# Six units of a mixer kernel with one more Strassen step each, and an earlier, split convolution epilogue

## The chip, the cores and the metric

The kernel runs on one core of one Trainium2 chip. The metric is the device time of that core in microseconds (us); the time of the kernel before is the median of three runs. A profile is of one execution, and its times count from the start of the profiled span.

## The reference

A decoder block on 256 tokens with a model width D of 4096, all in float32. A wide projection feeds two mixers of width 2048, a multi-scale causal pooling mixer and a gated short convolution, which are merged by sigmoid gates and projected out:

```
h    = rmsnorm(x, norm_w)
u_p, z_p, u_c, b_c, c_c, z_c, g = split(h @ w_in)     # 4096 -> 6 x 2048 + 2 x 4096
y_pool = (mix_g(trailing_mean_w(u_p) - u_p) * pool_scale) * silu(z_p)   # windows 2, 4, 8, 16
v      = c_c * u_c
y_conv = (b_c * (conv_b + sum_k conv_w[k] * shift(v, k))) * silu(z_c)   # 3 taps
merged = sum_n sigmoid(g_n + gate_b_n) * (y_n @ w_branch[n])            # n = pool, conv
out    = rmsnorm(x + merged @ w_out, final_norm_w)
```

## The kernel before, in words

**Units and steps.** The work is a list of units, each 1024 columns of a product's output. In order of time they are cz0 cb0 cu0 cc0, cz1 cb1 cu1 cc1 (the convolution's four projections, two halves), pz0 pu0 pz1 pu1 (the pooling's two), eight gate units that begin with g0_0 and end with g1_0, eight branch units b0_0 b1_0 ... b0_3 b1_3, and four output units o0 to o3. A unit of the wide products sums over 4096 rows in 16 steps of 256 rows; a branch unit has 8 steps. Each step is one block of weights, 256 rows by 1024 columns, that SP's queue fetches into `raw`, with an operand that stands on chip: the turned activations for the same 256 rows.

**Products in three.** Every float32 matrix is split into a rounded part (fp32r) and the rest, and a product of two takes three matmuls: high by high, high by low, low by high (L378). A matmul here is 128x512 by a 128x128 weight load. A step is of one of two kinds. P (plain) takes the 2 x 2 x 2 block products one by one: 8 x 3 = 24 matmuls. S (Strassen) takes seven products of sums of blocks: 7 x 3 = 21 matmuls. The order of an S step's products is written out in `groups`: N5 M2 N3 M1 N6 N7 N4; where S is the last step of a unit (`closing`) it is M2 N3 N4 M1 N7 N5 N6. N6, N4 and N7 use the sums of weight blocks that have to be formed first.

**Preparation.** A step's weights are prepared by two engines. ACT rounds the blocks into the ring, 26 cells of 128x512 (`highs`; its rows read ring<-raw and ring<-parts). DVE subtracts to get the rests (`lows`; ring<-raw,ring and ring<-parts,ring), and in an S step also forms the sums (`added` makes parts<-raw and parts<-raw,parts, `split` their rests). P takes 8 cells of the ring, S takes 14; where the cells wrap around the end of the ring, an operation is cut in two. An S step's fourth block (the corner) gets a second DMA of 256 KB on POOL's queue that adds a neighbour block to it (`issue_corner`). `pump` lets preparation run at most four steps ahead of TensorE (AHEAD) and issues a load when the buffer of the step four before is prepared; everything is recorded in program order on every engine.

**What sets the order.** A string of P and S for each unit, such as TEN = "PSPSSPSSPSSPSSPS", says which of its steps are Strassen steps. A unit's epilogue (activation, transposes, moves to DRAM) is a list of items in a queue. After each group of matmuls, `after_group` runs one item for every TICK = 6 matmuls; this count goes on across units. None in the list (`gap(n)` is n of them) lets ticks pass. So an item's place among the preparation steps on DVE and ACT is set by how many matmuls came before it. The convolution's epilogue `c_epi` belongs to cc0 and cc1 and runs while the next unit does, cz1 and pz0: it fetches the silu gate Y, transposes E on TensorE, lets 5 ticks pass, transposes Y, runs the taps (ACT, then `stt` on DVE at L76), and multiplies E = J * Y in one operation of 128x2048.

**Filling operands.** The operands of the branch and output units come back from DRAM by ACT's queue into the staging tiles sa, sb, sc, and are written into `arena` by the ticks (class `Fill`, `queue_fills`): for an S step's operand four sums on DVE (sb<-sb, 128x128 each), a rounding on ACT, and a subtraction on DVE (arena<-sb,arena, 896 or 1024 columns; 512 for a P step's). An operand can be filled once the steps that used its place are done. The order of the fills is the order in which the first unit that uses them, b0_0, b1_0 or o0, takes its steps.

In the views, TensorE's matmuls of steps are on L1063, DVE's tensor-tensor operations on L64 and ACT's on L61, since helpers record them; `sums` and `shared` are the two sets of four PSUM banks.

Of the kernel before, what the change touches and what calls it, by code (L numbers as in the profile page):

```python
# [18 lines left out]
HALF = D // 2  # L19
NU = 1024  # L20
# [12 lines left out]
WARM = 18  # L33
TAIL = 3

SIX5 = "PPPPPSPSPSPSPSPS"
FIRST = (0, 1, 8, 2, 9, 3, 10, 11, 4, 12, 13, 5, 14, 6, 15, 7)
OPENED = 12
SEVEN3 = "PPPSPSPSPSPSPSPS"
NINE = "PSPSPSPSSPSPSSPS"  # L40
NINE_A = "PSPSSPSPSSPSPSPS"
NINE_P = "PSPSSPSPSSPSSPSP"
HOST = "PPBPPMMPSSSPSSSPSSS"
SEVEN5 = "PPPPPSPSPSSPSSPS"
TEN = "PSPSSPSSPSSPSSPS"
OUT3 = "PSPSPSPSPSPSSPPP"
B0 = "PPPPSPSP"
B1 = "PSPSPSPP"
B1_FIRST = "PPSPSPSP"
B0_MORE = "PPPPSSPS"  # L50
# [3 lines left out]
def hybrid_block(ctx: ExitStack, tc: tile.TileContext, x, xc, prm, rows_in, w_in, pool_w, w_branch, w_out, out):  # L54
# [29 lines left out]
    def move(dst, src):  # L84
        return pin(nc.scalar.dma_start(dst, src))
# [410 lines left out]
    def gap(n):  # L496
        return [None] * n
# [68 lines left out]
    def conv_units(c, first):  # L566
        base = 2 * HALF + c * NU

        def b_epi(u):
            def product(t):  # L570
                stt(E[:, t], E[:, t], rin[:, t:t + 1], Y[:, t], ALU.mult, ALU.mult)
            return gap(15) + [lambda: product(0), None, lambda: product(1)] + gap(5) + [lambda: move(g_d[c], E)]

        def c_epi(u):
            def inner(j):
                if j == 3:
                    for i in range(4):
                        act(chan(E)[:, 2 * i:2 * i + 2], bankview(i))

            def outer(j):  # L580
                act(chan(J)[:, 2 * j:2 * j + 2], bankview(j))

            def taps(j):
                v, y = chan(E)[:, 2 * j:2 * j + 2], chan(Y)
                for i in range(2):
                    b = 2 * j + i
                    kb = 8 * c + b
                    act(y[:, b], v[:, i], AF.Identity, scale=tap_col(2, kb), bias=bias_col(kb))
                for s in (1, 2):
                    for i in range(2):  # L590
                        b = 2 * j + i
                        kb = 8 * c + b
                        stt(y[:, b, s:], v[:, i, 0:T - s], tap_col(2 - s, kb), y[:, b, s:], ALU.mult, ALU.add)

            items = gap(2) + [lambda: move(Y, g_d[c])] + gap(6) + pairs(transposes(E, inner)) + gap(5) + pairs(transposes(Y, outer))
            for j, n in enumerate((1, 3, 3, 3)):
                items += gap(n) + [lambda j=j: taps(j)]
            return items + [None, lambda: mul(chan(E), chan(J), chan(Y))] + gap(5) + [lambda: put(y_d[1, c], chan(E))]

        u = in_unit(f"cz{c}", base + 3 * HALF, lambda u: silu_y(u.late) + (gap(4) + side_items(ND - 1) + side_items(ND - 2) if first else []),  # L600
                    FIRST if first else SEVEN5, dst=Y)
        u.late = not first
        in_unit(f"cb{c}", base + HALF, b_epi, TEN if c else NINE_A).late = True
        u = in_unit(f"cu{c}", base, lambda u: rescale(Y), TEN, dst=Y)
        u.late = True
        in_unit(f"cc{c}", base + 2 * HALF, c_epi, TEN).urgent = lambda: mul(E, E, Y)

    def pool_units(c):
        u = in_unit(f"pz{c}", HALF + c * NU, lambda u: silu_y(True) + gap(4) + band_items(c), HOST if c else SEVEN5, dst=Y)
        u.late = True  # L610
        in_unit(f"pu{c}", c * NU, lambda u: [], NINE_P).urgent = lambda: None

# [94 lines left out]
    def gate_unit(n, c):  # L707
        first, final = (n, c) == (0, 0), (n, c) == (1, 0)

        def epi(u):  # L710
            d = u.dst

            def bias(t):
                gather(d[:, t], gate_b[n, None, c * NU:(c + 1) * NU].to_broadcast([P, NU]))

            def gate(t):
                act((spare() if final else d)[:, t], d[:, t], AF.Sigmoid)

            items = (rescale(d) if u.late else gap(1)) + [lambda: bias(0), None, None, lambda: bias(1)] + gap(12) + [
                lambda: gate(0), None, lambda: gate(1)]  # L720
            return items if first or final else items + gap(5) + [lambda: move(gates_d[n, c], E)]
        text = HOST if first else SEVEN3 if final else TEN
        u = in_unit(f"g{n}_{c}", 6 * HALF + n * D + c * NU, epi, text, dst=Y if first else E)
        u.late = not final

# [3 lines left out]
    def branch_unit(n, c):  # L729
        def epi(u):  # L730
            if n == 0:
                if c:
                    return gap(4) + [lambda: move(spare(), gates_d[1, c])] + gap(8) + [lambda: mul(Y, E, Y)]
                return gap(12) + [lambda: mul(Y, E, Y)]
            turned = spare() if c < 3 else Y

            def gated():
                mul(E, E, spare())
                if c == 3:
                    last_pair["stack"].close()  # L740
                    open_last(F32R)
                    last_pair["again"] = True

            def copy(j):
                act(chan(turned)[:, 2 * j:2 * j + 2], bankview(j))

            def stored():
                put(m_d[c], chan(turned))
                merged[c] = now[0] + STORED
            return gap(2) + [gated, None, lambda: add(E, E, Y), None,  # L750
                ] + gap(4) + pairs(transposes(E, copy)) + [
                    lambda: c < 3 and move(Y, gates_d[0, c + 1])] + gap(4) + [stored]

        text = (B1 if c else B1_FIRST) if n else B0_MORE if c else B0
        u = Unit(f"b{n}_{c}", lambda i: w_branch[n, c, i], seq_y(text), y_ops[n], epi)
        u.late = n == 0
        if not u.late:
            u.urgent, u.lead = (lambda: None), 3
        units.append(u)
# [3 lines left out]
    def out_unit(c):  # L763
        cs = slice(c * NU, (c + 1) * NU)

        def start():
            move(Y[:, 0], final_w[None, cs].to_broadcast([P, NU]))

        def epi(u):
            def row(t):  # L770
                gather(E[:, t], xrows[:, t, cs])

            def square(t):
                act(Y[:, 1], E[:, t], AF.Square, accum_out=ossq[:, t, c:c + 1])
            return gap(6) + [lambda: row(0), None, lambda: row(1)] + gap(3) + [start] + gap(11) + [
                lambda: square(0), None, lambda: square(1),
                lambda: mul(E, E, Y[:, 0:1].to_broadcast([P, 2, NU]))] + gap(4) + [lambda: move(o_d[c], E)]

        text = (SIX5, NINE, NINE, OUT3)[c]
        u = Unit(f"o{c}", lambda i: w_out[c, i], seq_x(text), m_ops, epi, before=start if c == 3 else None)  # L780
        u.late = c < 3
        units.append(u)
# [499 lines left out]
```

## Time and profile before

| what | before |
|---|---|
| median of three runs (lowest, highest) | 2353.83 us (2353.54, 2355.73) |
| the profiled execution, its span | 2353.71 us, 2352.0 us |
| TensorE (PE) busy | 2334.8 us, 99% of the span, 10400 matmuls |
| VectorE (DVE) busy | 2110.9 us, 90% |
| ScalarE (ACT) busy | 1528.8 us, 65% |
| GpSimd (POOL) busy | 293.1 us, 12% |
| DMA, mean | 269 GB/s, 633.01 MB |
| chain that ended last | PE 97%, DVE 1%, DMA 1% |

How to read it: the span is the time from the first to the last recorded instruction; an engine's busy time counts its working instructions, not those that issue DMAs. A row of the timeline has a start in us, a duration, the engine, the line, the operation, output <- inputs with shapes, a count, and in brackets the idle time just before it with what ended that. A row of the waits has the engine and its operation, the releaser, and then the sum of the waits in us, their number, and the longest. A row of the windows has the window's limits and length and then, for PE, PEld (weight loads), DVE, ACT and POOL, busy us with the number of instructions, the granted TensorE clock and the busy share of the DMA engines. The granted clock is 1.00 or just under it everywhere.

### The profile page before, as it was taken

How to read it: one execution, taken by the hardware profiler on the slowest of the kernel's cores; microseconds unless marked ns; L12 is line 12 of the kernel's file. 1: busy time of each engine (PE TensorE's matmuls, PEld its weight loads, DVE VectorE, ACT ScalarE, POOL GpSimd, SP SyncE). 2: the span in 40 equal slices, each digit the busy share in tenths (PEclk: the TensorE clock that was granted, in tenths of full speed). 3: DMA queues.
4: the chain of work that ended last, by engine and by line, in shares of the span. 5: the costliest groups of instructions: out<-in, count | busy, mean ns of one | idle time of the engine just before them, and what ended most of it. 6: DMA issues, size and time to landing. Idle time of an engine off the chain costs nothing.

```text
span 2352.0 us, 29771 instructions
## 1 busy us (share of the span) xinstructions
PE 2334.8 (99%) x10400; PEld 1931.9 (82%) x10400; DVE 2110.9 (90%) x2126; ACT 1528.8 (65%) x1897; POOL 293.1 (12%) x356
## 2 busy tenths in 40 slices
PE   9999999999999999999999999999999999999998
PEld 7888888888887888888888888888888888888886
DVE  8789998999989979979999899998898889999988
ACT  6666666666666666667666666666676566666664
POOL 0111100111101101101121111111011010011110
PEclk9999999999999999999999999999999999999999
DMA  9889877989977868868999999999889889889997
GB/s 377 245 249 295 269 235 238 277 243 288 270 231 231 255 203 256 252 207 256 295 276 273 303 284 285 277 312 278 285 259 288 272 253 304 270 235 303 283 264 288
DMA packets 202822, 633.01 MB, mean 269 GB/s; under 512 B 21296, under 2 KB 29744, under 8 KB 199856
## 3 DMA queue, kind: packets, MB, share of 16 engines
q1 hardware_dynamic: 134624, 485.42, 58.7%
q0 software_dynamic: 50400, 103.83, 24.2%
q10 hardware_dynamic: 17648, 41.87, 5.0%
q8 instruction: 81, 1.33, 0.2%
q14 instruction: 69, 0.57, 0.1%
HBM read 583.85 MB, written 25.17 MB: 259 GB/s over the span
## 4 chain that ended last, share of the span: by engine, by line
PE 97%; DVE 1%; DMA 1%; ACT 0%; issue 0%; SPq 0%; DVEq 0%; ACTq 0%
PE sums L1063 69%; PE shared L1063 26%; PE shared L692 1%; PE shared L477 1%; DMA raw<-in_w_in_dram 1%; ACT ring L61 0%; DVE parts L64 0%; DVE ring L64 0%; DVE Y L76 0%; PE shared L668 0%; PE shared L669 0%; PE shared L671 0%; SPq L79 0%; ACT Y L61 0%; PE shared L670 0%
## 5 line engine op out<-in xcount | busy, mean ns | idle before, releaser
L1063 PE MATMUL sums<-ring,arena 128*128 128x512 f32 x6873 | 1640.9, 390 | 4.7 <-DVE ring L64 4.2
L1063 PEld LDWEIGHTS sums<-ring,arena 128*128 128x128 f32 x6873 | 1287.2, 188 | 274.3 <-DVE ring L64 6.8
L64 DVE TENSOR_TENSOR ring<-raw,ring 128x1536 fp32r<-128x1536 f32 (+2 forms) x978 | 1088.4, 1138 | 146.5 <-PE sums L1063 49.3
L61 ACT ACTIVATE ring<-raw 128x512 fp32r<-128x512 f32 (+1 forms) x943 | 900.5, 1015 | 114.7 <-PE sums L1063 89.3
L61 ACT ACTIVATE ring<-parts 128x512 fp32r<-128x512 f32 (+1 forms) x478 | 389.2, 827 | 524.5 <-DVE parts L64 459.7
L1063 PE MATMUL shared<-ring,arena 128*128 128x512 f32 x2283 | 580.8, 389 | 0.2 <-DVE ring L64 0.2
L1063 PEld LDWEIGHTS shared<-ring,arena 128*128 128x128 f32 x2283 | 428.4, 188 | 89.6 <-DVE ring L64 0.6
L64 DVE TENSOR_TENSOR ring<-parts,ring 128x1536 fp32r<-128x1536 f32 (+2 forms) x262 | 404.7, 1555 | 15.8 <-ACT ring L61 8.1
L91 POOL DMA_DIRECT2D raw<-in_w_in_dram x176 | 152.2, 865 | 1375.7 <-DMA raw<-in_w_in_dram 535.7
L64 DVE TENSOR_TENSOR parts<-raw,parts 128x1024 f32<-128x1024 f32 x230 | 280.4, 1219 | 0.0
L64 DVE TENSOR_TENSOR parts<-raw 128x512 f32<-128x512 f32 x230 | 158.1, 687 | 2.7 <-DVE ring L64 0.7
L64 DVE TENSOR_TENSOR J<-J 128x512 f32<-128x512 f32 (+1 forms) x90 | 78.3, 870 | 15.5 <-ACT J L61 13.0
L1063 PE MATMUL sums<-ring,last_pair 128*128 128x512 f32 x306 | 76.5, 389 | 0.0
L61 ACT ACTIVATE J<-shared 128x512 f32<-128x512 f32 x128 | 68.5, 621 | 11.6 <-PE shared L1063 7.2
L61 ACT ACTIVATE E<-sums 128x512 f32<-128x512 f32 x76 | 42.1, 598 | 46.9 <-PE sums L1063 46.0
L1063 PEld LDWEIGHTS sums<-ring,last_pair 128*128 128x128 f32 x306 | 57.4, 188 | 12.0
L1063 PE MATMUL shared<-ring,side 128*128 128x512 f32 x261 | 66.0, 389 | 0.0
L91 POOL DMA_DIRECT2D raw<-in_w_out_dram x31 | 27.0, 872 | 264.9 <-DMA raw<-in_w_out_dram 112.7
L1063 PEld LDWEIGHTS shared<-ring,side 128*128 128x128 f32 x261 | 49.0, 188 | 10.2
L91 POOL DMA_DIRECT2D raw<-in_w_branch_dram x23 | 20.0, 870 | 288.9 <-DVE ring L64 104.1
L1063 PE MATMUL shared<-ring,last_pair 128*128 128x512 f32 x216 | 54.8, 389 | 0.0
L1063 PEld LDWEIGHTS shared<-ring,last_pair 128*128 128x128 f32 x216 | 40.5, 188 | 8.4
(123 smaller groups left out, 682.0 us busy)
## 6 DMA issues: line engine op xcount, KB each, us to landing
raw<-in_w_in_dram SPq DMA_DIRECT2D x318, 768.0 KB, 7.0
raw<-in_w_in_dram SPq DMA_DIRECT2D x326, 256.0 KB, 5.9
raw<-in_w_branch_dram SPq DMA_DIRECT2D x64, 768.0 KB, 6.7
raw<-in_w_out_dram SPq DMA_DIRECT2D x64, 768.0 KB, 6.6
raw<-in_w_in_dram POOLq DMA_DIRECT2D x176, 256.0 KB, 6.8
raw<-in_w_branch_dram SPq DMA_DIRECT2D x64, 256.0 KB, 5.5
raw<-in_w_out_dram SPq DMA_DIRECT2D x64, 256.0 KB, 5.6
E<-J POOLq DMA_DIRECT2D x30, 512.0 KB, 10.0
```

The costliest lines, as they stand in the source:

```text
L61: return pin(nc.scalar.activation(dst, src, func, **kw))
L64: return pin(nc.vector.tensor_tensor(out=dst, in0=a, in1=b, op=op))
L91: return pin(nc.gpsimd.dma_start(dst, src, accum_op=ALU.add))
L477: pin(nc.tensor.transpose(shared(j)[:, i * T + t * P:i * T + (t + 1) * P], src[:, t, c:c + P], ident))
L692: pin(nc.tensor.matmul(o, a, b, start=(k, i) == (0, 0), stop=(k, i) == (3, 2)))
L1063: pin(nc.tensor.matmul(ps, lhs, rhs, start=n == 0, stop=n == u.total[b] - 1))
```

## The change

Six strings are changed, each by one more S in the place of a P. For cz1 and pz0, "PPPPPSPSPSSPSSPS" becomes "PPPPSPSPSSPSSPSS"; the last gate unit g1_0 goes from "PPPSPSPSPSPSPSPS" to "PPPSPSPSPSSPSPSS"; o0 from "PPPPPSPSPSPSPSPS" to "PPPPPSPSPSSPSSPS"; o3 from "PSPSPSPSPSPSSPPP" to "PSPSSPSPSSPSSPPP"; and the first branch unit b0_0 from "PPPPSPSP" to "PPPPSSPS". The operands follow: in b0_0 the fifth, sixth and eighth step are now S steps, and an operand of o0 that was a P step's is an S step's. In `c_epi` the pause ahead of the transposes of Y is one tick and not five, and the product E = J * Y is two operations of 128x1024, two ticks apart.

```
-SEVEN3 = "PPPSPSPSPSPSPSPS"
+EIGHT3 = "PPPSPSPSPSSPSPSS"
...
-SEVEN5 = "PPPPPSPSPSSPSSPS"
+EIGHT4 = "PPPPSPSPSSPSSPSS"
...
-            items = gap(2) + [lambda: move(Y, g_d[c])] + gap(6) + pairs(transposes(E, inner)) + gap(5) + pairs(transposes(Y, outer))
+            items = gap(2) + [lambda: move(Y, g_d[c])] + gap(6) + pairs(transposes(E, inner)) + gap(1) + pairs(transposes(Y, outer))
...
-            return items + [None, lambda: mul(chan(E), chan(J), chan(Y))] + gap(5) + [lambda: put(y_d[1, c], chan(E))]
+            def whole(i):
+                b = slice(4 * i, 4 * i + 4)
+                mul(chan(E)[:, b], chan(J)[:, b], chan(Y)[:, b])
+
+            return items + [None, lambda: whole(0), None, None, lambda: whole(1)] + gap(5) + [lambda: put(y_d[1, c], chan(E))]
...
-                    FIRST if first else SEVEN5, dst=Y)
+                    FIRST if first else EIGHT4, dst=Y)
...
-        u = in_unit(f"pz{c}", HALF + c * NU, lambda u: silu_y(True) + gap(4) + band_items(c), HOST if c else SEVEN5, dst=Y)
+        u = in_unit(f"pz{c}", HALF + c * NU, lambda u: silu_y(True) + gap(4) + band_items(c), HOST if c else EIGHT4, dst=Y)
...
-        text = HOST if first else SEVEN3 if final else TEN
+        text = HOST if first else EIGHT3 if final else TEN
...
-        text = (B1 if c else B1_FIRST) if n else B0_MORE if c else B0
+        text = (B1 if c else B1_FIRST) if n else B0_MORE
...
-        text = (SIX5, NINE, NINE, OUT3)[c]
+        text = (SEVEN5, NINE, NINE, OUT3)[c]
```

(SEVEN5 and B0_MORE keep the strings that they have in the kernel before.) The helper lines move up by one: DVE's L64 and L76 are L63 and L75 after the change, ACT's L61 is L60.

What this does to the order of instructions is shown at two places. The first is DVE's order in pz0, from the last taps (Y<-E,par,Y) over the mul (E<-J,Y) to the rests of the step's sums (ring<-parts,ring); cz1 has the same piece. Before:

```order
L76 SCALAR_TENSOR_TENSOR Y<-E,par,Y 128x254 x2
L64 TENSOR_TENSOR E<-J,Y 128x2048
L64 TENSOR_TENSOR parts<-raw 128x512
L64 TENSOR_TENSOR ring<-raw,ring 128x512
L64 TENSOR_TENSOR parts<-raw,parts 128x1024
L64 TENSOR_TENSOR ring<-raw,ring 128x1536
L64 TENSOR_TENSOR ring<-parts,ring 128x1536
```

After:

```order
L75 SCALAR_TENSOR_TENSOR Y<-E,par,Y 128x254 x2
L63 TENSOR_TENSOR E<-J,Y 128x1024
L63 TENSOR_TENSOR parts<-raw 128x512
L63 TENSOR_TENSOR ring<-raw,ring 128x512
L63 TENSOR_TENSOR parts<-raw,parts 128x1024
L63 TENSOR_TENSOR E<-J,Y 128x1024
L63 TENSOR_TENSOR ring<-raw,ring 128x1536
L63 TENSOR_TENSOR ring<-parts,ring 128x1536
```

The second half of the mul has moved behind the first three operations of the S step, and stands ahead of its two wide ones.

The second is DVE's order near the end of o0: the last S steps' preparation, and with it the filling of the last operands (sb<-sb are the sums of one, arena<-sb,arena its rest). Before:

```order
L64 TENSOR_TENSOR ring<-raw,ring 128x1536
L64 TENSOR_TENSOR ring<-parts,ring 128x1536
L64 TENSOR_TENSOR sb<-sb 128x128 x4
L64 TENSOR_TENSOR ring<-raw,ring 128x1536
L64 TENSOR_TENSOR ring<-raw,ring 128x512
L64 TENSOR_TENSOR parts<-raw 128x512
L64 TENSOR_TENSOR ring<-raw,ring 128x512
L64 TENSOR_TENSOR parts<-raw,parts 128x1024
L64 TENSOR_TENSOR ring<-raw,ring 128x1536
L64 TENSOR_TENSOR ring<-parts,ring 128x1536
L64 TENSOR_TENSOR arena<-sb,arena 128x896
```

After:

```order
L63 TENSOR_TENSOR ring<-parts,ring 128x512
L63 TENSOR_TENSOR sb<-sb 128x128 x4
L63 TENSOR_TENSOR ring<-raw,ring 128x1536
L63 TENSOR_TENSOR ring<-raw,ring 128x512
L63 TENSOR_TENSOR parts<-raw 128x512
L63 TENSOR_TENSOR ring<-raw,ring 128x512
L63 TENSOR_TENSOR parts<-raw,parts 128x1024
L63 TENSOR_TENSOR ring<-raw,ring 128x1536
L63 TENSOR_TENSOR ring<-parts,ring 128x1536
L63 TENSOR_TENSOR arena<-sb,arena 128x1024
```

The rows are the same but for the last, which writes 1024 columns where it wrote 896, and for the wrap of the first.

More of the change, by code (lines that the diff above doesn't have):

```diff
@@ L34 @@
 TAIL = 3
-SIX5 = "PPPPPSPSPSPSPSPS"
+SEVEN5 = "PPPPPSPSPSSPSSPS"
 FIRST = (0, 1, 8, 2, 9, 3, 10, 11, 4, 12, 13, 5, 14, 6, 15, 7)
 OPENED = 12
-SEVEN3 = "PPPSPSPSPSPSPSPS"
+EIGHT3 = "PPPSPSPSPSSPSPSS"
 NINE = "PSPSPSPSSPSPSSPS"
@@ L43 @@
 HOST = "PPBPPMMPSSSPSSSPSSS"
-SEVEN5 = "PPPPPSPSPSSPSSPS"
+EIGHT4 = "PPPPSPSPSSPSSPSS"
 TEN = "PSPSSPSSPSSPSSPS"
-OUT3 = "PSPSPSPSPSPSSPPP"
-B0 = "PPPPSPSP"
+OUT3 = "PSPSSPSPSSPSSPPP"
 B1 = "PSPSPSPP"
```

## The prediction

> **What bounds the kernel now.** I read the page's totals first, then TensorE's waits, then the chain of waits. A change of 0.2% of this kernel, 4.7 us, is about what its measurement can tell from none.
>
> ```profile
> span 2352.0 us, 29771 instructions
> PE 2334.8 (99%) x10400; PEld 1931.9 (82%) x10400; DVE 2110.9 (90%) x2126; ACT 1528.8 (65%) x1897; POOL 293.1 (12%) x356
> PE sums L1063 <- DVE ring L64: 4.2, 3, 1.8
> PE shared L1063 <- DVE ring L64: 0.2, 1, 0.2
> 1591.54 16.32 PE sums L1063 x72
> ```
>
> TensorE is busy for 99% of the span. All of its waits for rounded operands sum to 4.4 us, each for DVE's writes to the ring. The last row is a piece of the chain: 72 matmuls in 16.32 us, 0.2267 us from one to the next. So the time is the number of matmuls times 0.2267 us, plus TensorE's waits, and DVE at 90% decides whether there are more of them.
>
> The stages that change, one row each (cz1, pz0, g1_0, b0_0, o0, o3): the window, its length, then busy PE, PEld, DVE, ACT, POOL, the granted clock, the DMA share:
>
> ```profile
> 336.06:423.34 87.28, 86.22 (x397) 71.31 (x395) 76.45 (x82) 55.25 (x75) 8.59 (x10) 1.00 0.79 240
> 664.06:752.68 88.62, 86.59 (x396) 71.21 (x395) 76.35 (x80) 55.44 (x74) 8.61 (x10) 1.00 0.79 238
> 1591.38:1673.66 82.28, 82.28 (x364) 68.13 (x363) 69.48 (x74) 54.52 (x66) 10.34 (x11) 1.00 0.96 293
> 1673.66:1715.82 42.16, 42.16 (x187) 34.91 (x186) 36.67 (x44) 30.38 (x40) 4.33 (x5) 1.00 0.83 259
> 2011.73:2096.54 84.81, 84.81 (x383) 70.34 (x382) 76.67 (x90) 53.23 (x66) 6.96 (x8) 1.00 0.82 250
> 2258.38:2340.80 82.42, 82.42 (x364) 67.94 (x362) 74.36 (x76) 47.75 (x61) 8.60 (x9) 1.00 0.86 273
> ```
>
> DVE is idle for 5.5 us in b0_0 and for 8 to 13 us in the others. Only cz1 and pz0 leave TensorE idle (1.1 and 2.0 us).
>
> **What a step costs.** The last stretch of o0 shows a P step and an S step on DVE:
>
> ```profile
> 2057.88 1.01 DVE L64 TENSOR_TENSOR sb<-sb 128x128 f32<-128x128 f32 x4
> 2058.80 1.01 DVE L64 TENSOR_TENSOR sc<-sc 128x128 f32<-128x128 f32 x4
> ...
> 2060.05 2.36 DVE L64 TENSOR_TENSOR ring<-raw,ring 128x1536 fp32r<-128x1536 f32 x2 [0.24 <-issue]
> 2064.12 1.23 DVE L64 TENSOR_TENSOR arena<-sb,arena 128x1024 fp32r<-128x1024 f32 x1 [1.71 <-ACT arena L61]
> ...
> 2082.95 2.35 DVE L64 TENSOR_TENSOR ring<-raw,ring 128x1536 fp32r<-128x1536 f32 x2
> 2085.22 0.68 DVE L64 TENSOR_TENSOR parts<-raw 128x512 f32<-128x512 f32 x1
> 2085.82 0.68 DVE L64 TENSOR_TENSOR ring<-raw,ring 128x512 fp32r<-128x512 f32 x1
> ...
> 2089.23 1.75 DVE L64 TENSOR_TENSOR ring<-parts,ring 128x1536 fp32r<-128x1536 f32 x1
> 2090.90 1.08 DVE L64 TENSOR_TENSOR arena<-sb,arena 128x896 fp32r<-128x896 f32 x1
> ```
>
> P takes DVE from 2082.95 to 2085.22, 2.27 us; S from 2085.22 to 2090.90, 5.68 us. Each of the six steps that turn from P to S therefore saves TensorE 3 matmuls (24 to 21), 0.68 us, and loads DVE with 3.41 us more. All six together save 18 x 0.2267 = 4.08 us, 0.17%. The rest of the sum is waits.
>
> [...]
>
> **cz1 and pz0.** TensorE's waits lie in the second S of a pair (step 10), in cz1 (first two rows) and pz0 (the rest):
>
> ```profile
> 392.06 0.84 PE L1063 MATMUL shared<-ring,arena 128*128 128x512 f32 x3
> 394.18 1.42 PE L1063 MATMUL sums<-ring,arena 128*128 128x512 f32 x5 [1.06 <-DVE ring L64]
> 720.16 0.39 PE L1063 MATMUL shared<-ring,arena 128*128 128x512 f32 x1
> 720.73 0.72 PE L1063 MATMUL shared<-ring,arena 128*128 128x512 f32 x2 [0.19 <-DVE ring L64]
> 721.30 0.40 PE L1063 MATMUL sums<-ring,arena 128*128 128x512 f32 x1
> 723.54 1.43 PE L1063 MATMUL sums<-ring,arena 128*128 128x512 f32 x5 [1.84 <-DVE ring L64]
> ```
>
> In cz1 the fifth matmul of step 10 was due at 392.06 + 4 x 0.2267 = 392.97 and came at 394.18, 1.21 us late; after such a wait the next matmul is some 0.11 us late too (from 720.73 to 721.30 two take 0.57 us for 0.45). Together 1.3 us. In pz0 step 11 starts 21 x 0.2267 = 4.76 us after 720.16 if nothing waits; the second matmul is late by 0.35 us, the fifth by a further 2.01, with 0.22 behind them: 2.6 us.
>
> ```profile
> 364.82 1.76 DVE L76 SCALAR_TENSOR_TENSOR Y<-E,par,Y 128x255 f32<-128x255 f32 x4 [3.16 <-ACT Y L61]
> ...
> 387.83 2.29 DVE L64 TENSOR_TENSOR E<-J,Y 128x2048 f32<-128x2048 f32 x1
> 390.04 0.68 DVE L64 TENSOR_TENSOR parts<-raw 128x512 f32<-128x512 f32 x1
> ...
> 394.05 1.75 DVE L64 TENSOR_TENSOR ring<-parts,ring 128x1536 fp32r<-128x1536 f32 x1
> 693.60 1.76 DVE L76 SCALAR_TENSOR_TENSOR Y<-E,par,Y 128x255 f32<-128x255 f32 x4 [3.83 <-ACT Y L61]
> ...
> 723.40 1.75 DVE L64 TENSOR_TENSOR ring<-parts,ring 128x1536 fp32r<-128x1536 f32 x1
> L64 DVE TENSOR_TENSOR parts<-raw,parts 128x1024 f32<-128x1024 f32 x230 | 280.4, 1219 | 0.0
> ```
>
> DVE was idle (3.16, 3.83 us) until the first taps, which wait through ACT for TensorE's transposes, and then works nearly without a break to the rounded rests that step 10 wants: 29.2 us in cz1, 29.8 in pz0. The change takes out one P step before this stretch, which brings step 10's work one step (24 matmuls, 4 ticks of 6) forward, and moves the transposes 4 ticks forward (gap of 5 to 1). So taps, mul and rests keep their places to each other and to TensorE, and the idle time ahead of the taps is not used: in the order, the same rows lie between taps and rests. The mul's second half is also issued ahead of those rests, so that splitting it frees nothing. It costs a little: two starts of 1.14 us (the 1.22 us form less the 0.08 us by which starts overlap) for one of 2.21 (387.83 to the next start at 390.04), 0.07 us. In cz1 two writes no longer wrap around the ring; a write of 1536 columns takes 1.67 us to the next start (2089.23 to 2090.90), in pieces of 1024 and 512 columns 1.14 + 0.60, 0.07 more. So its wait stays, less 0.1 us. The bounds are 0 and 2.7: a stretch that begins later by the mul's half.
>
> In pz0 the ticks themselves move. They count matmuls by six without regard to units, and cz1 lost 3, so every tick in pz0 falls 3 matmuls, 0.68 us, earlier. From the first taps to step 10, TensorE then has cz1's 392.06 - 364.82 = 27.24 us, where pz0 had 720.16 - 693.60 = 26.56. With the same work as cz1, pz0's wait becomes cz1's 1.3 plus 0.07, say 1.4: 1.2 us gained (bounds: nothing, and all 2.6).
>
> [...]
>
> The new pair S, S at the end of each unit: the last S forms its third operand's rest (product N4) for the eighth matmul. DVE ended step 14's rests before that step started, so it runs 5.7 us from there; the step after starts 4.76 later and wants it at 4.76 + 1.59. It is covered by 0.6 us; uncovered it costs at most 3.4.
>
> **g1_0 and b0_0.** In g1_0 the last stretch holds the added S and also the fill of the operand that b0_0 now uses as its fifth.
>
> ```profile
> 1637.53 0.68 DVE L64 TENSOR_TENSOR arena<-sc,arena 128x512 fp32r<-128x512 f32 x1
> ...
> 1647.40 2.36 DVE L64 TENSOR_TENSOR ring<-raw,ring 128x1536 fp32r<-128x1536 f32 x2 [1.24 <-ACT E L61]
> ...
> 1666.52 1.01 DVE L64 TENSOR_TENSOR sa<-sa 128x128 f32<-128x128 f32 x4
> 1668.90 2.20 PE L1063 MATMUL sums<-ring,arena 128*128 128x512 f32 x9
> 1678.13 2.68 DVE L64 TENSOR_TENSOR J<-J 128x512 f32<-128x512 f32 x3 [3.89 <-ACT J L61]
> ```
>
> From 1637.53 to the end of the last S, 1666.52, DVE works 28.99 - 1.24 = 27.75 us. Added: 3.41, a fill's four sums 0.92 (sb's in o0, 2057.88 to 2058.80) and its subtraction of 1024 columns 1.14, less one of 512 columns that moves behind, 0.60 (2085.22 to 2085.82). That makes 32.6, ending at 1670.2. Step 15 starts at 1668.90 - 0.68 = 1668.22 and wants it at 1669.81: 0.4 us with the late matmul behind (0 to 1.5). In b0_0 the added 3.41 us meet 5.5 us idle, of which 3.89 lie ahead of everything, and 1 us of filling has moved out in front: nothing (0 to 1).
>
> **o0.** Here the order of the fills decides. Step 15 is an S step before and after; its operand is the last one filled.
>
> ```profile
> 2086.31 5.60 PE L1063 MATMUL sums<-ring,last_pair 128*128 128x512 f32 x24
> 2091.75 2.23 PE L1063 MATMUL sums<-ring,arena 128*128 128x512 f32 x9
> ```
>
> Before, the operand's low half was written at 2090.90 to 2091.98, and the third matmul, the first that reads it, ran at 2091.75 + 0.45 = 2092.20: in time by 0.2 us. After, step 15 starts 0.68 earlier and wants it at 2091.52. DVE's stretch from 2057.88 to that write was 33.02 us with 1.95 idle (0.24 and 1.71, which backlog now fills), 31.07 of work. With one S for a P (3.41), the wide and a narrow operand's subtraction exchanged (1024 columns for 896, 1.23 for 1.08, which moves the start of the last by -0.15) and two wraps fewer (-0.14) it is 34.2: the write starts at 2092.1, takes 1.23, ends at 2093.3. TensorE waits 1.8, with the late matmul 1.9 us. Bounds: 0, should DVE find 2 us more, and 3.4, the whole S.
>
> **o3.** The S is inside the alternation, 8 us are idle, and TensorE's last matmuls start 0.68 earlier behind the same tail: nothing (0 to 0.5).
>
> **Sum:** -4.1 (matmuls) - 0.1 (cz1) - 1.2 (pz0) + 0.4 (g1_0) + 1.9 (o0) = -3.1 us. The profiled execution took 2353.71 us (span 2352.0 and 1.7 around it), 0.1 under the median of 2353.83; from the median the forecast is 2350.7 us.
>
> **The rivals.** *The late operand of o0 is not waited for*: if DVE gains 2 us in that stretch. For it: the estimate is a sum of 34 us with small margins, and it was in time before. Against it: that margin was 0.2 us. -3.1 - 1.9 = -5.0: 2348.8 us. Chance 0.22.
>
> *Both old waits go*, as splitting the mul and pulling the transposes forward would have it if DVE's idle 3 us ahead of the taps were used. Against it: the order above. -3.1 - 2.6 = -5.7: 2348.1 us. Chance 0.08.
>
> *DMA decides*: each S fetches another 256 KB corner, and g1_0 stands at 0.96 of the DMA engines. A corner that is late by one step's 2 us costs that: 2352.7 us. For TensorE no wait on a DMA is listed now. Chance 0.10.
>
> *DVE sets the pace*: if the idle time in the table above lies where the added work cannot use it, each S costs 3.41 - 0.68 = 2.73 us, six of them 16.4: 2370.2 us. It decides from the point where DVE ends a last S later than the eighth matmul, 1.6 us into the step, unit after unit. For it: 90% and the waits all being DVE's. Against: 5.5 us or more idle in every window. Chance 0.05.
>
> **The numbers.** The forecast holds 0.55, with its own range 2349.2 to 2352.4. To hold 8 in 10, the range runs from 2347.8 (the two better cases) to 2353.2 (DMA, and the upper bounds of g1_0 and b0_0); the pace case stays outside. Faster by over 4.7 us, under 2349.1: both better cases and little of the forecast's edge, 0.31. Slower by as much, above 2358.5: most of the pace case, 0.04. Between: 0.65.
>
> **What would show it.** 10382 matmuls at 0.227 us; the wait in cz1's step 9 still 1.2 us, in pz0's step 9 about 1.3 and one instead of two; a new wait of 1.8 us at the start of o0's step 15, released by DVE's arena write and not by the ring; 0.3 in g1_0's step 15. No such wait in o0, or waits in steps that follow the pairs S, S, or any wait on a DMA, would prove the sum wrong.

## The result

The changed kernel takes 2361.14 us (median of 8 runs, 2359.37 to 2362.34), the kernel before beside it 2353.76 us (2353.44 to 2355.84): 7.4 us more. The ratio computed from the same runs is 1.0028 with a 95% interval of 1.0019 to 1.0037, which is 6.6 us. The runs of the kernel before fall into two groups 1.5 us apart (last section); six of these eight lie in the lower one. The forecast was 2350.7 us in a range of 2347.8 to 2353.2; it went the other way. One of the ten runs of e1 below took 4557.02 us at a granted clock of 0.883, and it is left out of e1's ratio.

The profiled execution took 2360.14 us, with a span of 2358.3. Its page begins:

```profile
span 2358.3 us, 29787 instructions
PE 2336.2 (99%) x10382; PEld 1930.9 (82%) x10382; DVE 2131.4 (90%) x2138; ACT 1537.4 (65%) x1903; POOL 299.0 (13%) x362
```

The 18 matmuls are gone (10400 to 10382), as forecast, and TensorE's busy time is 1.4 us longer nevertheless. So time was lost in waits, and some matmuls were slower. TensorE's waits in the changed kernel (releaser, sum, number, longest; the first 10 us of the span, with 1.9 us of waits now and 1.6 before, are left out):

```profile
PE sums L1066 <- DVE ring L63: 4.8, 5, 1.4
PE shared L1066 <- DVE ring L63: 2.2, 1, 2.2
PE sums L1066 <- ACT arena L60: 1.4, 1, 1.4
PE sums L1066 <- DVE arena L63: 0.5, 1, 0.5
```

Before they summed to 4.4 us, all for the ring; now to 8.9. The next view has the units in order of time, cz1, pz0, g1_0, b0_0, b1_0, o0, o3: the window and its length, busy time of PE, PEld, DVE, ACT, POOL, the granted clock, the DMA share. The last row is b1_0 in the kernel before, which the prediction didn't show:

```profile
336.30:423.00 86.70, 85.55 (x393) 70.76 (x392) 79.75 (x85) 56.87 (x77) 8.63 (x10) 1.00 0.80 243
663.80:750.50 86.70, 85.56 (x393) 70.73 (x392) 79.71 (x85) 56.73 (x77) 8.62 (x10) 1.00 0.80 244
1589.49:1673.07 83.58, 82.17 (x362) 67.40 (x360) 72.61 (x77) 55.85 (x68) 11.24 (x12) 1.00 0.91 281
1673.07:1718.97 45.90, 43.67 (x184) 35.45 (x183) 39.33 (x46) 30.38 (x40) 5.23 (x6) 0.96 0.85 258
1718.97:1761.66 42.69, 41.89 (x184) 34.20 (x183) 41.37 (x43) 28.19 (x37) 4.24 (x4) 1.00 0.87 255
2016.10:2103.60 87.50, 85.28 (x381) 69.51 (x380) 80.32 (x92) 55.68 (x68) 7.82 (x9) 1.00 0.83 247
2265.40:2347.20 81.80, 81.77 (x361) 67.38 (x359) 77.61 (x79) 49.14 (x63) 8.63 (x9) 1.00 0.87 280
```
```profile
1715.82:1757.34 41.52, 41.52 (x185) 34.38 (x184) 40.76 (x48) 27.99 (x37) 4.26 (x4) 1.00 0.87 263
```

Against the windows of before: cz1 -0.6, pz0 -1.9, o3 -0.6, as forecast; but g1_0 +1.3, b0_0 +3.7, b1_0 +1.2 and o0 +2.7. That is 5.8 of the 6.3 us by which the span grew; the rest is 0.1 or 0.2 us each in other units. Only b0_0 has a granted clock under 1.00.

**What happens in b0_0.** First POOL's queue in the kernel before, then POOL's queue, the chain of waits and ACT in the changed one:

```profile
1685.87 0.87 POOL L91 DMA_DIRECT2D E<-in_rows_dram  x1 [4.95 <-DVE E L76]
```
```profile
1687.38 0.86 POOL L90 DMA_DIRECT2D raw<-in_w_branch_dram  x1 [8.49 <-DMA raw<-in_w_branch_dram]
1687.96 2.06 POOL L90 DMA_DIRECT2D E<-in_rows_dram  x2
```
```profile
1687.96 12.84 DMA E<-in_rows_dram
```
```profile
1700.82 1.06 ACT L60 ACTIVATE last_pair<-E 128x1024 f32<-128x1024 f32 x1 [6.91 <-DMA E<-in_rows_dram]
1701.79 1.56 ACT L60 ACTIVATE ring<-parts 128x512 fp32r<-128x512 f32 x2
```

Three S steps have three corners on POOL's queue ahead of the two transfers that add the last gate unit's bias (E<-in_rows), where there were two, and the third stands there until its block has come. So the first bias transfer leaves 14.9 us into b0_0 (1687.96), where it left after 12.2 before (1685.87), and lands 12.84 us later. It also takes longer. Shortest, middle and longest time of the two bias transfers, before and changed; the shortest is the first one's:

```profile
DMA to landing us min/median/max: 8.7/10.3/12.0
DMA to landing us min/median/max: 12.8/14.8/16.8
```

The bias thus lands 6.9 us later in the unit, 2.7 from the later start and 4.2 from the longer transfer. The corner ahead of it on the queue had left 0.58 us earlier and landed only at 1696.38. That this company on the queue makes the bias transfer longer, 12.8 us for the 8.7 before, was not tested by itself. ACT's sigmoid (last_pair<-E) waits 6.91 us for it. Behind the sigmoid in ACT's order stand the roundings of the new step's sums (ring<-parts); DVE needs them for the rests, and TensorE needs those:

```profile
1705.19 1.61 PE L1066 MATMUL shared<-ring,arena 128*128 128x512 f32 x5 [2.23 <-DVE ring L63]
1706.60 5.74 PE L1066 MATMUL sums<-ring,arena 128*128 128x512 f32 x18
```
```profile
1705.20:1710.00 4.80, 4.80 (x14) 3.84 (x15) 4.76 (x9) 4.14 (x6) 0.86 (x1) 0.64 0.59 155
```

TensorE is idle for 2.23 us, and with late matmuls around it 2.7 us are lost. Then the granted clock is 0.64 on average over 4.8 us: the matmuls from 1707.02 to 1709.58 start 0.427 us apart in place of 0.227, and 14 take 4.80 us where 3.17 would do, another 1.6. Together that is 4.3 of the 4.4 us that b0_0 lost beyond its saving (3.7 + 0.7).

### The profile page after: what moved, and what is told of

Its sections match the earlier page's. It is cut to its first block, busy times and chain, and to the rows that moved or that the text cites. A ratio compares the mean times of both kernels' runs of the same rounds, so it can differ in the third digit from the quotient of the medians.

```text
span 2358.3 us, 29787 instructions
## 1 busy us (share of the span) xinstructions
PE 2336.2 (99%) x10382; PEld 1930.9 (82%) x10382; DVE 2131.4 (90%) x2138; ACT 1537.4 (65%) x1903; POOL 299.0 (13%) x362
## 4 chain that ended last, share of the span: by engine, by line
PE 96%; DVE 2%; DMA 1%; ACT 1%; issue 0%; DVEq 0%; ACTq 0%; SPq 0%; POOL 0%; POOLq 0%
PE sums L1066 67%; PE shared L1066 26%; DVE ring L63 1%; PE shared L695 1%; PE shared L476 1%; DMA E<-in_rows_dram 1%; DVE parts L63 0%; ACT ring L60 0%; DMA raw<-in_w_branch_dram 0%; DMA raw<-in_w_in_dram 0%; DVE arena L63 0%; DVE E L63 0%; PE shared L671 0%; PE shared L672 0%; PE shared L674 0%
## 5 line engine op out<-in xcount | busy, mean ns | idle before, releaser
L63 DVE TENSOR_TENSOR ring<-raw,ring 128x512 fp32r<-128x512 f32 (+2 forms) x970 | 1088.5, 1146 | 137.3 <-PE sums L1066 57.7
L60 ACT ACTIVATE ring<-raw 128x1536 fp32r<-128x1536 f32 (+1 forms) x935 | 899.1, 1021 | 95.0 <-PE sums L1066 74.7
L60 ACT ACTIVATE ring<-parts 128x1024 fp32r<-128x1024 f32 (+1 forms) x492 | 398.9, 824 | 536.0 <-DVE parts L63 478.5
L1066 PE MATMUL shared<-ring,arena 128*128 128x512 f32 x2307 | 587.6, 389 | 2.2 <-DVE ring L63 2.2
L63 DVE TENSOR_TENSOR ring<-parts,ring 128x1536 fp32r<-128x1536 f32 (+2 forms) x269 | 415.3, 1554 | 17.1 <-ACT ring L60 16.7
L63 DVE TENSOR_TENSOR parts<-raw,parts 128x1024 f32<-128x1024 f32 x236 | 287.6, 1219 | 0.0
L63 DVE TENSOR_TENSOR parts<-raw 128x512 f32<-128x512 f32 x236 | 162.1, 687 | 2.2
L63 DVE TENSOR_TENSOR J<-J 128x512 f32<-128x512 f32 (+1 forms) x90 | 78.2, 869 | 13.3 <-ACT J L60 10.8
L60 ACT ACTIVATE J<-shared 128x512 f32<-128x512 f32 x128 | 68.3, 621 | 7.1 <-PE shared L1066 6.8
L60 ACT ACTIVATE E<-sums 128x512 f32<-128x512 f32 x76 | 41.9, 597 | 45.2 <-PE sums L1066 44.5
L1066 PE MATMUL shared<-ring,last_pair 128*128 128x512 f32 x264 | 66.5, 389 | 0.0
L1066 PE MATMUL sums<-ring,last_pair 128*128 128x512 f32 x246 | 63.6, 391 | 1.4 <-DVE ring L63 1.4
L1066 PEld LDWEIGHTS shared<-ring,last_pair 128*128 128x128 f32 x264 | 49.6, 188 | 10.3
L1066 PEld LDWEIGHTS sums<-ring,last_pair 128*128 128x128 f32 x246 | 45.9, 188 | 12.1 <-DVE ring L63 2.6
```

The source lines that it names most:

```text
L60: return pin(nc.scalar.activation(dst, src, func, **kw))
L63: return pin(nc.vector.tensor_tensor(out=dst, in0=a, in1=b, op=op))
L1066: pin(nc.tensor.matmul(ps, lhs, rhs, start=n == 0, stop=n == u.total[b] - 1))
```

## The experiments

The working theory after this trace: the z units and o3 gain what was forecast. The loss lies with g1_0, b0_0, b1_0 and o0, where an engine stands in its own order behind something that waits for a transfer or a filled operand. The rivals: the extra transfers slow the kernel everywhere, or DVE simply has too much to do in these units. Medians are compared with those of the kernel before in the same batch: 2354.36 us (e1 to e4), 2354.83 (e5 to e8), 2355.07 (e9 to e12). Where kernels of different batches are set against each other, these 0.7 us are the uncertainty.

**e1: the z units and o3 alone**: the changed kernel with the other three strings as before.

```
...
-        text = HOST if first else EIGHT3 if final else TEN
+        text = HOST if first else SEVEN3 if final else TEN
...
-        text = (B1 if c else B1_FIRST) if n else B0_MORE
+        text = (B1 if c else B1_FIRST) if n else B0_MORE if c else B0
...
-        text = (SEVEN5, NINE, NINE, OUT3)[c]
+        text = (SIX5, NINE, NINE, OUT3)[c]
```

> Only cz1, pz0 (with the earlier and split epilogue) and o3 are changed; g1_0, b0_0 and o0 are as before. Theory (the loss lies in g1_0, b0_0, b1_0 and o0, where late operands and a late gate hold TensorE): these three units keep what the changed kernel's trace shows of them, -0.5, -1.9 and -0.7 us, so 3.1 us under the kernel before, 2350.7 us, with one wait of 1.3 us in each z unit's tenth step. Rival (the extra corner transfers slow the kernel everywhere): the gain is gone, within 1 us of before or above it.

2350.95 us, ratio 0.9984 (0.9975 to 0.9994), 3.4 under before where the theory had 3.1. The extra corners of these units cost nothing that shows.

**e2: b0_0 alone**, on the kernel before.

```
-        text = (B1 if c else B1_FIRST) if n else B0_MORE if c else B0
+        text = (B1 if c else B1_FIRST) if n else B0_MORE
```

> Only b0_0 has its third S step. In the order, ACT's first sigmoid of g1_0 (last_pair<-E) now stands behind the roundings of the sixth step's sums (ring<-parts), where in the changed kernel it stands ahead of them; the new corner's transfer is ahead of the bias transfers on POOL's queue in both. Theory (TensorE waits in b0_0 because ACT waits for the bias with those roundings behind it): no wait over 0.5 us in b0_0, so 0.7 us less there, and at most the 1.1 us wait of b1_0: 2353.0 to 2354.3 us. Rival (DVE has too much to do in b0_0 with three S steps): the wait of 2.5 us and the slow matmuls behind it are there all the same, 3.5 to 4.5 us over before, 2357.3 to 2358.3 us.

2358.26 us (2355.28 to 2360.05), ratio 1.0017 (1.0007 to 1.0026). Half and half: the profiled execution, the fastest of its runs, has no wait at all in b0_0, as the place of the sigmoid demands, and late matmuls of 1.7 us in b1_0; but the median, 3.9 over before, is where the rival had it.

**e3: the sigmoid one tick later**, on the changed kernel.

```
-            items = (rescale(d) if u.late else gap(1)) + [lambda: bias(0), None, None, lambda: bias(1)] + gap(12) + [
+            items = (rescale(d) if u.late else gap(1)) + [lambda: bias(0), None, None, lambda: bias(1)] + gap(13 if final else 12) + [
```

> The changed kernel with g1_0's two sigmoids one tick later (a pause of 13 ticks and not 12), which puts both behind the roundings of b0_0's sixth step on ACT; nothing else moves. Theory (ACT's place of the sigmoid): b0_0 loses its wait of 2.5 us and the 1.7 us by which the matmuls behind it are slow, 4.2 us under the changed kernel, 2357 us. Rival (DVE's load in b0_0): as the changed kernel, 2361 us.

2357.16 us (2356.41 to 2359.84): 4.0 under the changed kernel, and 2.8 over before in place of 7.4. ACT now runs the roundings first; the first sigmoid then finds its bias, and the second waits 1.30 us for its own without harm:

```profile
1697.28 1.06 ACT L60 ACTIVATE ring<-parts 128x1024 fp32r<-128x1024 f32 x1 [1.10 <-DVE parts L63]
1698.24 1.99 ACT L60 ACTIVATE ring<-raw 128x1536 fp32r<-128x1536 f32 x2
1700.14 1.04 ACT L60 ACTIVATE last_pair<-E 128x1024 f32<-128x1024 f32 x1
...
1704.39 1.06 ACT L60 ACTIVATE last_pair<-E 128x1024 f32<-128x1024 f32 x1 [1.30 <-DMA E<-in_rows_dram]
```
```profile
1671.95:1713.50 41.55, 41.55 (x185) 34.36 (x183) 38.20 (x46) 29.25 (x37) 5.23 (x6) 1.00 0.94 284
```

b0_0 takes 41.55 us with TensorE busy throughout and a clock of 1.00. The transfers are as long as in the changed kernel (17.3 us from the first's leaving to the second's landing: 1687.06 to 1704.39, there 1687.96 to 1705.30), so this shows the cause of the wait in b0_0: one place in ACT's order. Only b0_0's share is settled by it; g1_0, b1_0 and o0 still wait here.

**e4: o0 alone**, on the kernel before.

```
-        text = (SIX5, NINE, NINE, OUT3)[c]
+        text = (SEVEN5, NINE, NINE, OUT3)[c]
```

> Only o0 has its seventh S step. Theory (the last operand filled is late for step 15, and DVE's backlog also makes the two steps ahead late): waits of 2.3 to 3.4 us in steps 13 to 15 against 0.7 us of matmuls saved, 1.6 to 2.7 us over before, 2355.4 to 2356.5 us. Rival (o0's waits in the changed kernel come from the backlog that b0_0 and b1_0 hand on): without that, at most the one wait of 1.9 us that was forecast, 1.2 us over before or less, under 2355.1 us.

2359.47 us, ratio 1.0021 (1.0011 to 1.003), 5.1 over before. Worse than the theory, and the rival is refuted: without any backlog from earlier units, o0 has every wait of the changed kernel, and one at step 10 as well. TensorE's rows at steps 10, 13 and 15:

```profile
2070.12 1.43 PE L1063 MATMUL sums<-ring,arena 128*128 128x512 f32 x5 [1.08 <-DVE ring L64]
...
2086.01 1.42 PE L1063 MATMUL sums<-ring,arena 128*128 128x512 f32 x5 [0.38 <-DVE ring L64]
...
2097.21 0.73 PE L1063 MATMUL sums<-ring,arena 128*128 128x512 f32 x2 [1.40 <-ACT arena L61]
2098.47 2.57 PE L1063 MATMUL sums<-ring,arena 128*128 128x512 f32 x7 [0.53 <-DVE arena L64]
```

Both halves of the last operand are late. The seven matmuls of the last row take 2.57 us, where the changed kernel's took 1.88 for the same: the slow clock again (0.68 from 2100.0 to 2104.5), which explains part of the surplus; step 10 is the other part.

**e5: b0_0 alone, without the last gate unit's bias.**

```
-            items = (rescale(d) if u.late else gap(1)) + [lambda: bias(0), None, None, lambda: bias(1)] + gap(12) + [
+            items = (rescale(d) if u.late else gap(1)) + ([None] * 4 if final else [lambda: bias(0), None, None, lambda: bias(1)]) + gap(12) + [
```

> As the run with b0_0's third S step alone, but the last gate unit's bias is left out (its two accumulating transfers into E are not issued, so the gate g1_0 lacks its bias); the order on ACT and DVE is the same. Theory (what most runs of that kernel lose beyond its profiled one is time in which ACT waits for the bias): 0.7 us of matmuls saved and the waits in b1_0 of 1.1 to 1.7 us, 2354.5 to 2355.5 us, with a spread no wider than that of the kernel before. Rival (DVE's load alone): as with the bias, 2358 us and as wide.

2357.31 us (2355.82 to 2360.33), 1.0 under e2: the theory fails here. Most of what the runs of e2 lose is not the bias. The profile, of the slowest of the ten runs, shows another transfer of the same kind: DVE stands in b1_0 before Y = E * Y until the accumulating transfer of b0_0's corners (E<-J, on POOL's queue) has landed, and TensorE pays for it:

```profile
1745.68 2.29 DVE L64 TENSOR_TENSOR Y<-E,Y 128x2048 f32<-128x2048 f32 x1 [1.89 <-DMA E<-J]
```
```profile
1752.64 2.50 PE L1063 MATMUL sums<-ring,arena 128*128 128x512 f32 x5 [2.45 <-DVE ring L64]
```

In this execution slow matmuls followed the wait as well, here (five in 2.50 us) and in pz0 (nine in 3.65), at 1.4 and 1.6 us; e2's profile, of its fastest run, has neither, so they may be part of why the runs of both spread so far.

**e6: g1_0 alone**, on the kernel before.

```
-SEVEN3 = "PPPSPSPSPSPSPSPS"
+SEVEN3 = "PPPSPSPSPSSPSPSS"
```

> Only g1_0 has its eighth S step. Theory (DVE's backlog at the end of the unit, with the pauses for ACT not absorbed): a wait of 1.3 to 2.0 us at its last step against 0.7 us of matmuls saved, 0.6 to 1.3 us over before, 2354.7 to 2355.4 us. Rival (in the changed kernel this wait is there because b0_0's S operand is filled earlier): no wait, 0.7 us under before, 2353.4 us.

2355.34 us, ratio 1.0003 (0.9993 to 1.0012). The rival is right about the wait, though its 2353.4 us was met by one run alone (2353.55; the other nine have 2355.07 to 2356.51): TensorE doesn't wait in g1_0,

```profile
1592.90:1674.50 81.60, 81.60 (x361) 67.57 (x360) 71.88 (x77) 56.32 (x69) 11.09 (x12) 1.00 0.94 291
```

and the unit is 0.7 us shorter than before (82.28). Nor does it in e9, where of g1_0, b0_0 and o0 only b0_0 is changed. So it takes both to make g1_0's last step late: the eighth S step, and b0_0's new operand, which is filled at the end of g1_0. A run with these two alone was not made. What g1_0 saves alone is given back in o0: the ticks fall 3 matmuls otherwise, and its last operand, which had been in time by 0.2 us, costs 0.56. e2 and e5, which also take 3 matmuls out ahead of o0, and e9 and e10, which take 9, show the same; e1, e7 and e11, which take 6, a whole tick, don't.

Alone, the parts give -3.4 us (e1), +0.5 (e6), +3.9 (e2) and +5.1 (e4); their sum is +6.1.

**e7: half of the product behind the rests**, on e1.

```
-            return items + [None, lambda: whole(0), None, None, lambda: whole(1)] + gap(5) + [lambda: put(y_d[1, c], chan(E))]
+            return items + [None, lambda: whole(0)] + gap(4) + [lambda: whole(1)] + gap(5) + [lambda: put(y_d[1, c], chan(E))]
```

> The kernel with cz1, pz0 and o3 changed, and the second half of the product E = J * Y two ticks later, which puts it behind the rests of the tenth step's sums on DVE; all else is the same. Theory (those rests are late by what DVE does ahead of them): each wait of 1.3 us shrinks by the half's 1.14 us to 0.2 us, 2.3 us under that kernel, 2348.7 us. Rival (the rests wait for ACT or the half only meets the next pair of S steps): within 0.5 us of 2350.95 us.

2349.59 us (2349.14 to 2349.99), ratio 0.9978 (0.9969 to 0.9988). In the profile the matmul that waited is late by 0.18 and 0.16 us in place of 1.3 and 1.3, as expected; 0.25 us turn up at the step behind, so that 1.4 of the expected 2.3 us are left.

**e8: o0 with seven S steps in alternation**, on the kernel before.

```
-        text = (SIX5, NINE, NINE, OUT3)[c]
+        text = (SEVEN3, NINE, NINE, OUT3)[c]
```

> The kernel before with seven S steps in o0 in strict alternation, PPPSPSPSPSPSPSPS, so that the pairs S, S are gone and the fills fall elsewhere; the same last operand. Theory (in o0 the fills and the second S of a pair meet on DVE, and the last operand is late besides): the waits of steps 10 and 13 go, the one of step 15 stays at 1 to 2.5 us: 0.3 to 1.8 us over before, 2354.7 to 2356.2 us. Rival (DVE has no room for a seventh S step in this unit, wherever it is put): waits as with the pairs, 5 us over before, 2359 us. If the late operand was a matter of the pairs as well: 0.7 us under before.

2355.84 us, ratio 1.0005 (0.9995 to 1.0014). The waits of the pairs are gone, and the last operand is late all the same, by less:

```profile
2093.72 0.73 PE L1063 MATMUL sums<-ring,arena 128*128 128x512 f32 x2 [0.22 <-ACT arena L61]
2094.98 1.90 PE L1063 MATMUL sums<-ring,arena 128*128 128x512 f32 x7 [0.53 <-DVE arena L64]
```

So the theory's two parts stand: pairs that meet the fills, and an operand filled last. DVE can carry a seventh S step in o0 at a loss of 1 us, but nothing is gained by it.

**e9: b0_0's S step on e7**, where no z unit disturbs the view.

```
-        text = (B1 if c else B1_FIRST) if n else B0_MORE if c else B0
+        text = (B1 if c else B1_FIRST) if n else B0_MORE
```

> The best kernel so far (cz1, pz0, o3, the half product behind the rests; 2349.6 us) with b0_0's third S step as well. Its z units have no wait long enough for the slow clock, so what b0_0 costs is seen clearly. Theory (DVE stands in b1_0 before Y = E * Y until the accumulating transfer E<-J has landed, with the rests of b1_0's seventh step queued behind it): 0.7 us of matmuls saved, waits of 1 to 4.9 us in b1_0 from run to run, 2350.5 to 2354 us and a spread of 2 us or more. Rival (the spread of that run came from pz0 alone): within 0.7 us of 2350.3 us, spread under 1 us.

2353.17 us (2352.39 to 2354.19), 3.6 over e7 (3.3 by the kernel before beside each), spread 1.8 us: within the theory's time, a little under its spread; the rival's 2350.3 is out.

**e10: the product in b1_0 two ticks later**, on e9.

```
-                return gap(12) + [lambda: mul(Y, E, Y)]
+                return gap(14) + [lambda: mul(Y, E, Y)]
```

> As the kernel beside it, with b1_0's product Y = E * Y two ticks later (a pause of 14 ticks and not 12), which puts it behind the rests of the seventh step on DVE. Theory (the product's wait for its transfer): the wait in b1_0's seventh step is gone, only that of 0.7 us at its first step is left, 2349.5 to 2350.3 us, spread under 1.2 us. Rival (DVE's load): as the kernel beside it.

2352.0 us: 1.2 under e9, as much as the matmul at the seventh step was late (1.2 us in e9's profile), which is gone. The theory's 2349.5 to 2350.3 is missed all the same: b1_0's first step keeps 1.9 us, not 0.7, and o0 has its 0.55 us as in e6. ACT still stands 1.1 us before the sigmoid for the bias, and the next steps' roundings behind it are late by that; whether this is all of the 1.9 us was not tried. The third S step in b0_0 costs 2.4 us net over e7 even so.

**e11: both halves of E = J * Y behind the pair**, on e1.

```
-            return items + [None, lambda: whole(0), None, None, lambda: whole(1)] + gap(5) + [lambda: put(y_d[1, c], chan(E))]
+            return items + gap(8) + [lambda: whole(0), None, None, lambda: whole(1)] + gap(5) + [lambda: put(y_d[1, c], chan(E))]
```

> cz1, pz0 and o3 changed, and both halves of E = J * Y later: the first behind the tenth step's rests and the eleventh step's, the second behind the twelfth step's. Theory (what DVE does ahead of a pair's second S step is what TensorE waits for): the 0.28 us at step 10 and the 0.36 us behind it go in each z unit, unless the pair behind (steps 12 and 13) now gets them: 2348.3 us if they go, 2349.6 us if they only move. Rival (the rests wait for something else): 2349.6 us with the same waits in the same places.

2348.31 us (2348.13 to 2348.61), ratio 0.9973 (0.9962 to 0.9984): the time of the first case, and the fastest kernel here. TensorE is busy through both z units:

```profile
336.20:421.50 85.30, 85.30 (x393) 70.73 (x392) 79.54 (x84) 56.34 (x76) 8.52 (x10) 1.00 0.80 245
662.30:747.60 85.30, 85.30 (x393) 70.72 (x392) 79.53 (x85) 56.37 (x76) 8.19 (x10) 1.00 0.80 244
```

**e12: the kernel before with only the product split**, and its second half later.

```
-            return items + [None, lambda: mul(chan(E), chan(J), chan(Y))] + gap(5) + [lambda: put(y_d[1, c], chan(E))]
+            def whole(i):
+                b = slice(4 * i, 4 * i + 4)
+                mul(chan(E)[:, b], chan(J)[:, b], chan(Y)[:, b])
+
+            return items + [None, lambda: whole(0)] + gap(4) + [lambda: whole(1)] + gap(5) + [lambda: put(y_d[1, c], chan(E))]
```

> The kernel before without any new S step; only E = J * Y is split, with the second half behind the rests of the second S step of the pair. Theory: the waits of cz1 and pz0 shrink by 1.1 us each, and pz0's is then too short for the slow clock, so that the slower half of the runs of before is gone: 2351.3 to 2351.8 us, spread under 1 us. Rival (the gain of the kernel with the half product behind came from its S steps alone): within 0.5 us of the kernel before.

2351.95 us (2351.11 to 2352.4), ratio 0.9988 (0.9979 to 0.9998): 3.1 under before, 0.15 over the theory's range, spread 1.3. DVE's order alone thus gives 3.1 of the 5.2 us that e7 gains; the nine matmuls of its three S steps, 2.0 us at 0.2267 each, make up the rest.

## Why the prediction was wrong

- **What bounds the kernel** held, but for the slow clock behind a wait (1.6 us in b0_0): matmuls times 0.2267 us plus waits for operands. What failed is the sum of the waits. Against the forecast the windows are longer by 4.4 us in b0_0, 1.2 in b1_0, 1.6 in g1_0, 1.5 in o0 and 0.2 in cz1, which turns -3.1 into the 5.8 measured.
- **cz1 and pz0** held. One wait is left in each, at step 9, of 1.15 and 1.14 us idle, 1.4 each with the late matmuls (the prediction had 1.2 and 1.4), and the order was read rightly: e7 and e11 show that the product ahead of the rests is what keeps it. Split, it costs 382.73 to 383.86 and 386.20 to 387.34, 2.27 us for 2.21, so the 0.07 taken from the starts is right:

```profile
382.73 1.22 DVE L63 TENSOR_TENSOR E<-J,Y 128x1024 f32<-128x1024 f32 x1
383.86 0.68 DVE L63 TENSOR_TENSOR parts<-raw 128x512 f32<-128x512 f32 x1
...
386.20 1.21 DVE L63 TENSOR_TENSOR E<-J,Y 128x1024 f32<-128x1024 f32 x1
387.34 1.75 DVE L63 TENSOR_TENSOR ring<-raw,ring 128x1536 fp32r<-128x1536 f32 x1
```

- **"In b0_0 the added 3.41 us meet 5.5 us idle ... nothing (0 to 1)"** is the step that failed. It counted DVE's work against DVE's idle time, and never looked at what the new step's other instructions stand behind. The corner's transfer is one more entry ahead of the bias on POOL's queue, and the roundings of its sums stand on ACT behind a sigmoid that waits for the bias. Measured: 4.3 us in b0_0, 1.6 of them slow matmuls, such as followed pz0's wait of 1.84 us in four traces of six (last section), and 1.1 us in b1_0, a unit that the sum left out. There DVE comes late with its backlog and has the product Y = E * Y ahead of the seventh step's rests; the wait for E<-J is 0.1 us in this execution (1747.51 to 1747.63), and up to 1.89 in e5's. The rival *DMA decides* had the right resource and the wrong place: not a corner late by one step, but an epilogue's transfer, late and longer, with a step's roundings queued behind its reader.
- **g1_0**: forecast 0.4, measured 1.9. The work was sized rightly (32.6 us forecast; 33.95 with two pauses of 0.55 and 0.70 make 32.7), but the sum took the old pause out and put none in. The new ones are waits for ACT's rounding, which itself waits for its turn on ACT. Ahead of the first pause stands what b0_0 showed: a sigmoid (E<-E) that waits for the bias of the gate unit before, with the roundings behind it. That bias lands after 17.3 us, where it took 13.3 before and ACT had no wait. Whether the wait of 1.41 us goes without it was not tried. ACT, DVE and TensorE:

```profile
1645.86 1.06 ACT L60 ACTIVATE E<-E 128x1024 f32<-128x1024 f32 x1 [1.18 <-DMA E<-in_rows_dram]
...
1647.35 1.56 ACT L60 ACTIVATE ring<-parts 128x512 fp32r<-128x512 f32 x2
```
```profile
1648.94 1.76 DVE L63 TENSOR_TENSOR ring<-parts,ring 128x1536 fp32r<-128x1536 f32 x1 [0.55 <-ACT ring L60]
...
1661.81 1.23 DVE L63 TENSOR_TENSOR arena<-sb,arena 128x1024 fp32r<-128x1024 f32 x1 [0.70 <-ACT arena L60]
```
```profile
1668.10 2.40 PE L1066 MATMUL sums<-ring,last_pair 128*128 128x512 f32 x8 [1.41 <-DVE ring L63]
```

- **o0**: the wait at step 15 was forecast and is there, 2.5 us with late matmuls for 1.9; the prediction's rival without it is refuted. The stretch was sized rightly: 2062.72 to 2097.85, less a pause of 0.69 for ACT, is 34.4 us of work for 34.2, and the pause was again not in the sum. But the forecast named the wrong releaser for most of it: TensorE waits 1.40 us for ACT's rounding of the operand (arena<-sb) and only then 0.53 for the write by DVE that the forecast named. The rounding runs at 2096.78, 7.6 us after its sums were ready on DVE (2089.21), behind two roundings of weights. Steps 13 and 14 add 0.8 us that no term stood for; three operands' sums now run in a row on DVE ahead of a pair, where there were two:

```profile
2062.72 1.01 DVE L63 TENSOR_TENSOR sb<-sb 128x128 f32<-128x128 f32 x4
2063.64 1.01 DVE L63 TENSOR_TENSOR sa<-sa 128x128 f32<-128x128 f32 x4
2064.57 1.01 DVE L63 TENSOR_TENSOR sc<-sc 128x128 f32<-128x128 f32 x4
...
2097.85 1.22 DVE L63 TENSOR_TENSOR arena<-sb,arena 128x1024 fp32r<-128x1024 f32 x1 [0.69 <-ACT arena L60]
```
```profile
2094.89 1.99 ACT L60 ACTIVATE ring<-raw 128x1536 fp32r<-128x1536 f32 x2
2096.78 1.04 ACT L60 ACTIVATE arena<-sb 128x1024 fp32r<-128x1024 f32 x1
```
```profile
2097.87 0.73 PE L1066 MATMUL sums<-ring,arena 128*128 128x512 f32 x2 [1.40 <-ACT arena L60]
2099.13 1.88 PE L1066 MATMUL sums<-ring,arena 128*128 128x512 f32 x7 [0.53 <-DVE arena L63]
```

- **o3** held, and so did the saving by matmuls.
- **The chances**: "slower by over 0.2%" got 0.04, from DVE's pace alone. No case stood for several units each giving back more than they save, which is what came.

## What to carry over

An added step has to be followed in the order of every engine and queue that it uses: ask what its new instructions stand behind, and what that waits for; idle time of the engine with the most work doesn't answer it. An epilogue's operation that can wait, a reader of a transfer above all, should stand behind the roundings and rests that the next steps need: moving it there was worth 4.0 us (e3), 1.2 (e10), 1.4 (e7) and 2.6 (e11), each more than the 0.68 us of an added S step. Pauses of an engine for a neighbour belong in the sum of a stretch unless it is shown that the neighbour can run ahead.

## What the runs showed of the hardware

After the same wait TensorE's matmuls were slow in some executions and not in others. pz0's old wait of 1.84 us (idle) is the same to the hundredth in six traces, those of the kernel before and of e2, e4, e5, e6 and e8, which have the unit unchanged. What follows is not: the next nine matmuls into shared take 2.20 and 2.21 us in the kernel before and e2, and 3.65, 3.50 and 3.81 in e5, e6 and e8; in e4 the five ahead of them take 2.50 us, where they take 1.43 in the kernel before, and the clock is 0.65 from 724.5 to 728.5. First the kernel before, then e8, over the same stretch behind it:

```profile
724.80:728.90 4.10, 4.10 (x20) 3.39 (x19) 4.10 (x7) 2.69 (x4) 0.53 (x1) 1.00 1.01 324
```
```profile
724.80:728.90 4.10, 4.10 (x13) 3.19 (x12) 4.10 (x7) 2.76 (x4) 0.72 (x1) 0.58 1.01 313
```

20 matmuls at a clock of 1.00, or 13 at 0.58: seven fewer, 1.6 us. In o0 waits of 1.40 and 0.53 us, two matmuls apart, were followed by a clock of 0.68 in e4 (2100.0 to 2104.5), and of 1.00 in the changed kernel (2099.0 to 2104.0). The runs of the kernel before fall into two groups about 1.5 us apart (2353.8 to 2354.4 and 2354.9 to 2356.3 us beside e9 to e12), and e7 and e11, which have no wait of that length there, spread by 0.9 and 0.5 us; that the groups are this clock is inferred: the mean clock of a whole run is 0.998 in all thirteen of the lower one, and 0.997 in six of the fifteen of the upper. Idle times of 1.84 and 2.23 us stood ahead of slow matmuls here, 0.427 us from one to the next in b0_0; those of 1.15, 1.14 and 1.41 us in the changed kernel's cz1, pz0 and g1_0 were followed by a clock of 1.00.
